# Attention scores as three split products, values held stationary, and the overflow branch ahead of the first pair of experts

## The chip, the cores and the metric

One core of a Trainium2 chip runs the whole kernel. The metric is the device time of one execution in microseconds (us), lower is better. The kernel's engines are TensorE (PE in the profile; PEld are its weight loads), VectorE (DVE), ScalarE (ACT), GpSimd (POOL) and SyncE (SP), which issues the large transfers.

## What is computed

Two transformer blocks follow each other. The first has two layers over 256 latent and 256 context tokens of width 1024; the second has one layer over the 256 latent tokens. A layer of the first block mixes tokens in three branches and then sends each token to two of 32 experts. Cut to what matters here:

```python
def diff_softmax_mix(q, k, v, lam):                 # 4 heads, two maps of 64 each
    s = einsum('bqhmd,bkhmd->bhmqk', q, k) * 64 ** -0.5
    p = softmax(s, axis=-1)
    w = p[:, :, 0] - lam * p[:, :, 1]
    return einsum('bhqk,bkhe->bqhe', w, v)

def neighbourhood_attention(q, k, v, k_ctx, v_ctx, rpb, rows):   # 8 heads of 64
    s = concatenate([s_window + bias, s_ctx], axis=-1)           # scaled scores
    p = softmax(s, axis=-1)
    return p_window @ v_window + p_ctx @ v_ctx

def hier_moe(x, ...):      # 2 of 32 experts for a token, 1024 -> 512 -> 1024
    hdn = silu(xb @ w_gate[e]) * (xb @ w_up[e])
    return hdn @ w_down[e]                          # times the token's weight, summed

def rope(x, pos):          # second block, dilated branch: cos and sin of pos * inv
```

All inputs and the output are fp32.

## The kernel before

**Dense products.** A weight arrives in fp32 and is split into a high and a low part of type fp32r (L153 on ScalarE, L155 on VectorE). Activations are kept split as well (`xh`, `xl`), so a dense product is three fp32r matmuls per piece: high by high, low by high, high by low (L229 to L231, L247 to L249). An fp32 matmul, where there is one, is carried out as two instructions, which the profile counts as two records.

**Attention.** In `mix`, q and k are kept as fp32 tiles `qT` and `kT`, features on partitions, two heads (or the two maps of a head) in the two halves of the partitions. A pair of score matmuls (L618 in the differential attention, L675 in the neighbourhood attention) uses each half as a row tile of 64 rows: 128 queries by 512 keys for latent tiles, 256 keys for context tiles. Layer 0 works on four token tiles (two latent, two context), layer 1 on the two latent ones. VectorE takes the maximum (L621, L691, with the bias added at L689), ScalarE the exponential (L624, L694, L696, L702), TensorE transposes the weights in blocks of 128 (L137, `T`), ScalarE copies them out as `wT` (L635, L708), and TensorE multiplies them with the values (L637, L710). At L710 the weights `wT` (128 keys by 128 queries) are loaded and the values of one head (64 columns) move; the sums are divided by the softmax sums at L712 and L713 for a whole token tile. `to_yT` (L717) then transposes the result. For each latent pair four small transfers on POOL's queue bring the bias tile `bt` (L686); `bt`, `wT` and other tiles share four buffers (tag `t2`).

The order of instructions on an engine comes from the framework's scheduler, by readiness and program order. Dense pieces of the next products stand between the steps of the attention. A helper, `issue_after(x)`, queues the instructions of its block behind `x`, those on `x`'s engine alone.

**Experts.** For each layer `load` (L1016) brings the weights of two experts in six transfers of 2 MB on SP's queue: two of gate, two of up, two of down. They go into buffers in turn (L949 to L954): seven in layer 0, nine in layer 1. `choose` and `gather` make the matrix of chosen tokens for four experts (L1022, L1048; for the first four L1038); `expert_pair` multiplies two experts at once in two column tiles of 64 (L966 with L968 for gate and up, L990 with L992 for down), and `scatter` (L1082, L1083) adds the result to the tokens. Eight groups of two pairs follow each other, their TensorE order being program order; the `scatter` of a pair is issued inside the next one, and the next group's `gather` inside the second pair (`fill`, L1195) except in the first group. `overflow` (L1112) is a branch on the largest count of tokens of an expert: its body, which works through tokens beyond 64 of an expert with a loop, is not entered for these inputs. Every engine loads the count (L1114) and takes the branch (L1115). It stands behind the first group (L1211): there the last `scatter` is drained, a down buffer is given to the body, the load of that buffer is issued after it (L1212), and the next group's `gather` follows.

**Rope tables.** `rope_tables` (L1336) makes cosines and sines for block 2's dilated branch. It is called in the idle time of the first norm (`idle`, L1729), two transfers for it in the setup.

Of the kernel before, what the change touches and what calls it, by code (L numbers as in the profile page):

```python
# [8 lines left out]
FT = mybir.dt.float32  # L9
BF = mybir.dt.bfloat16  # L10
FR = mybir.dt.float32r
I32 = mybir.dt.int32
# [77 lines left out]
class Builder:  # L90
# [173 lines left out]
    def setup(self, st, open_mix, load_x):  # L264
# [23 lines left out]
        with self.tp("setup", 1) as tp:  # L288
# [4 lines left out]
            inv = self.p_h.tile([128, 64], FT, name="inv2")  # L293
            nc.gpsimd.dma_start(inv, I["k_inv"])
            pi = self.p_h.tile([128, 2], I32, name="pi")
            nc.gpsimd.dma_start(pi, I["positions_2"][0].rearrange("(t p) -> p t", p=128))
            self.rope_in = inv, pi
# [110 lines left out]
    def mix_norm(self, tp, l, h, mid=None, junk=None, idle=None):  # L408
# [6 lines left out]
        for w in range(2):  # L415
            y = tp.tile([128, 2, D], FT, name="xs", tag="xs", bufs=2)
            r = self.stats(h, (2 * w, 2 * w + 1), y[:, 0] if junk is None else junk)
            if w == 0 and self.spare:
                self.fence.append(self.sq)
            for k in range(2):  # L420
                scaled = nc.vector.tensor_scalar(y[:, k], h[:, 2 * w + k], r[:, k:k + 1], None, op0=OP.mult)
            xs.append(y)
        if idle is not None:
            with self.tc.issue_after(scaled.ins):
                idle()
# [81 lines left out]
    def mix(self, l, xh, xl):  # L507
# [80 lines left out]
        rope = at.tile([128, 256], FT, name="rope")  # L588
        nc.gpsimd.dma_start(rope, I["k_rope"])

        def ev_qk(dst):
            def ev(t, ps):
# [8 lines left out]
                nc.scalar.activation(dst[:, :, t * 128:(t + 1) * 128], pt.rearrange("p (c t) -> p c t", c=4), AF.Copy)  # L601
# [5 lines left out]
        for t in tts:  # L607
# [4 lines left out]
            for h in range(4):  # L612
                S = [self.aux() for _ in range(2)]
                mx, nm, sm = (self.small(2, f"da{x}") for x in "xns")
                P = at.tile([128, 2, 512], FT, name="P", tag="P", bufs=2)
                for m in range(2):
                    r0 = m * 64
                    mm(S[m][:, :nk], lhsT=qT[r0:r0 + 64, h, t * 128:(t + 1) * 128], rhs=kT[r0:r0 + 64, h, k0:],  # L618
                       start=True, stop=True)
# [3 lines left out]
                for m in range(2):  # L623
                    nc.scalar.activation(P[:, m, :nk], S[m][:, :nk], AF.Exp, bias=nm[:, m:m + 1], scale=0.125,  # L624
                                         accum_out=sm[:, m:m + 1])
# [34 lines left out]
        self.dense_w(W(O_KC), 8, 512, xh, xl, 512, lambda c, ps: nc.scalar.activation(kT[:, c], ps, AF.Copy))  # L660
        self.dense_w(W(O_QC), 8, 512, xh, xl, n, lambda c, ps: nc.scalar.activation(qT[:, c, :n], ps[:, :n], AF.Copy))
        self.dense_x(W(O_VC), 8, 512, xh, xl, allt, lambda t, ps: nc.scalar.activation(v[:, t], ps, AF.Copy))
        yc = at.tile([128, 4, 512], FT, name="ytok", tag="ytok")
        for t in tts:
            po = self.aux()
            sm = self.small(8, "nsm")
# [3 lines left out]
            for h in range(8):  # L670
                c, r0 = h // 2, (h % 2) * 64
                if h % 2 == 0:
                    S2 = [self.aux() for _ in range(2)]
                    for m in range(2):
                        mm(S2[m][:, :nk], lhsT=qT[m * 64:m * 64 + 64, c, t * 128:(t + 1) * 128],  # L675
                           rhs=kT[m * 64:m * 64 + 64, c, k0:], start=True, stop=True)
                S = S2[h % 2]
                P = at.tile([128, 2, 512], FT, name="PC", tag="P", bufs=2)[:, 0]
                mx, nm, ps2 = (self.small(2, f"na{x}") for x in "xns")
                if lat:  # L680
                    if h % 2 == 0:
                        bt = at.tile([128, 2, 4, 64], FT, name="bt", tag="t2", bufs=4)
                        for u in range(2):
                            off = h * 889 + (3 - (2 * t + u)) * 127 + 63
                            for k in range(2):
                                nc.gpsimd.dma_start(bt[u * 64:(u + 1) * 64, k], bass.AP(  # L686
                                    tensor=self.d_bias.tensor, offset=self.d_bias[l].offset + off + k * 889,
                                    ap=[[7111, 64], [127, 4], [1, 64]]))
                    nc.vector.tensor_tensor_reduce(P[:, :256], S[:, :256], bt[:, h % 2].rearrange("p a b -> p (a b)"),  # L689
                                                   1.0, -3e38, OP.add, OP.max, mx[:, 0:1])  # L690
                    nc.vector.tensor_reduce(mx[:, 1:2], S[:, 256:], axis=AX.X, op=OP.max)  # L691
                    nc.vector.tensor_tensor(mx[:, 0:1], mx[:, 0:1], mx[:, 1:2], op=OP.max)
                    nc.vector.tensor_scalar(nm[:, 0:1], mx[:, 0:1], -0.125, None, op0=OP.mult)
                    nc.scalar.activation(P[:, :256], P[:, :256], AF.Exp, bias=nm[:, 0:1], scale=0.125,  # L694
                                         accum_out=ps2[:, 0:1])
                    nc.scalar.activation(P[:, 256:], S[:, 256:], AF.Exp, bias=nm[:, 0:1], scale=0.125,  # L696
                                         accum_out=ps2[:, 1:2])
                    nc.vector.tensor_tensor(sm[:, h:h + 1], ps2[:, 0:1], ps2[:, 1:2], op=OP.add)
                else:
                    nc.vector.tensor_reduce(mx[:, 0:1], S[:, :nk], axis=AX.X, op=OP.max)  # L700
                    nc.vector.tensor_scalar(nm[:, 0:1], mx[:, 0:1], -0.125, None, op0=OP.mult)
                    nc.scalar.activation(P[:, :nk], S[:, :nk], AF.Exp, bias=nm[:, 0:1], scale=0.125,  # L702
                                         accum_out=sm[:, h:h + 1])
                pt = self.aux()
                for b in range(nk // 128):
                    self.T(pt[:, b * 128:(b + 1) * 128], P[:, b * 128:(b + 1) * 128])
                wT = at.tile([128, 512], FT, name="wT", tag="t2", bufs=4)
                nc.scalar.activation(wT[:, :nk], pt[:, :nk], AF.Copy)  # L708
                for b in range(nk // 128):
# [50 lines left out]
    def tail(self, l, mh, ml, h_src, hook, emit):  # L760
# [426 lines left out]
        for bt in range(8):  # L1187
            PTw = []
            with in_order():
# [645 lines left out]
```

## Time and profile before

| | |
|---|---|
| median of 3 runs | 2613.09 us |
| lowest, highest | 2610.91, 2614.15 us |
| the profiled execution | 2611.69 us |
| its span in the trace | 2609.9 us |
| mean granted clock of TensorE | 0.98 |

The stages in that span, in rounded us: layer 0's mixing 30 to 610 (differential attention 183 to 300, neighbourhood attention 382 to 510), its projection and routing to 690, its experts 690 to 1183; layer 1's mixing 1200 to 1520 (differential attention 1286 to 1352, neighbourhood attention 1404 to 1497), projection and routing to 1573, experts 1573 to 2032; block 2 from 2040 to 2610.

In the rows below, times are us unless marked ns. A row of a timeline gives the start, the time until the last of its instructions ends, the engine, the line, the operation and how many. The ends of matmuls are modelled, so that one overlaps the next by a little. A row of groups gives the busy time, the mean of one instruction in ns, and the idle time of the engine ahead of it with what released it. A row of windows gives for each engine the busy time and instructions in a stretch.

### The profile page before, as it was taken

Reading aid. Unit: us, or ns where it says so; the run is one execution under the profiler, and the core shown is the slowest. Engines: PE = TensorE matmul, PEld = TensorE weight load, DVE = VectorE, ACT = ScalarE, POOL = GpSimd, SP = SyncE. Lnnn points to the kernel's source line nnn. Section 1 sums busy time; section 2 is a strip of 40 time slices with the busy share of each in tenths; the row PEclk is TensorE's granted clock in tenths of the full one; section 3 lists DMA queues with packets and bytes.
Section 4 is the critical chain, followed back from the end, with each engine's and each line's share of the span. In section 5 each row is a group of like instructions: output and inputs, shape, how many; then the busy total and the mean of one; then the engine's idle time right before and its main releaser. Section 6 shows DMA issues by size and latency. Waiting matters only on the chain. (4 is left out here: it accounts for less than half of the span.)

```text
span 2609.9 us, 33466 instructions
## 1 busy us (share of the span) xinstructions
PE 2471.3 (95%) x13560; PEld 1686.8 (65%) x13560; DVE 1309.2 (50%) x2640; ACT 852.0 (33%) x1504; POOL 163.2 (6%) x187
## 2 busy tenths in 40 slices
PE   7999999999889999997999978999898899998998
PEld 5766776677544444545878774444342798897997
DVE  5635523346444444548553463233232686657784
ACT  4334333424211111115444441111110534444663
POOL 1200002011200000003000210000000100001000
PEclk9999999999899999998999999999999999999999
DMA  9743544263889999985243478999999435535452
GB/s 316 214 162 114 169 146 122 93 209 149 329 342 417 419 417 418 418 356 193 73 133 104 139 300 328 421 421 421 421 421 413 164 119 194 177 122 184 152 188 99
DMA packets 177363, 652.47 MB, mean 250 GB/s; under 512 B 15174, under 2 KB 18778, under 8 KB 127666
## 3 DMA queue, kind: packets, MB, share of 16 engines
q1 hardware_dynamic: 169682, 626.97, 62.4%
q0 software_dynamic: 7520, 23.29, 3.0%
q8 instruction: 109, 1.79, 0.3%
q14 instruction: 52, 0.43, 0.0%
HBM read 644.42 MB, written 5.80 MB: 249 GB/s over the span
## 5 line engine op out<-in xcount | busy, mean ns | idle before, releaser
L155 DVE TENSOR_TENSOR wl<-raw,wh 128x1024 fp32r<-128x1024 f32 (+1 forms) x279 | 335.8, 1207 | 310.9 <-ACT wh L153 305.3
L966 PE MATMUL acc<-raw,xg 128*64 128x512 f32 x896 | 399.0, 596 | 19.6 <-DMA raw<-in_moe_w_up 10.1
L153 ACT ACTIVATE wh<-raw 128x1024 fp32r<-128x1024 f32 (+1 forms) x288 | 299.0, 1045 | 334.9 <-PE acc L248 167.3
L968 PE MATMUL acc<-raw,xg 128*64 128x512 f32 x896 | 399.2, 596 | 0.0
L247 PE MATMUL acc<-xh,wh 128*128 128x256 f32 (+1 forms) x1184 | 370.6, 315 | 0.0
L248 PE MATMUL acc<-xl,wh 128*128 128x256 f32 (+1 forms) x1184 | 369.5, 313 | 0.0
L249 PE MATMUL acc<-xh,wl 128*128 128x256 f32 (+1 forms) x1184 | 368.5, 312 | 0.1
L966 PEld LDWEIGHTS acc<-raw,xg 128*64 128x64 f32 x896 | 119.8, 137 | 273.4 <-issue 247.2
L247 PEld LDWEIGHTS acc<-xh,wh 128*128 128x128 f32 x1184 | 226.3, 192 | 28.1 <-issue 13.8
L248 PEld LDWEIGHTS acc<-xl,wh 128*128 128x128 f32 x1184 | 226.4, 191 | 15.8 <-issue 5.9
L249 PEld LDWEIGHTS acc<-xh,wl 128*128 128x128 f32 x1184 | 225.9, 191 | 11.7 <-issue 1.0
L229 PE MATMUL acc<-wh,xh 128*128 128x512 f32 x544 | 214.0, 394 | 5.0 <-DVE xh L441 2.5
L230 PE MATMUL acc<-wl,xh 128*128 128x512 f32 x544 | 213.6, 393 | 0.3 <-DVE wl L155 0.3
L231 PE MATMUL acc<-wh,xl 128*128 128x512 f32 x544 | 213.8, 394 | 0.0
L990 PE MATMUL acc<-raw,hT 128*64 128x512 f32 x472 | 209.8, 596 | 3.0 <-ACT hT L982 3.0
L992 PE MATMUL acc<-raw,hT 128*64 128x512 f32 x472 | 209.8, 596 | 0.0
L997 DVE TENSOR_TENSOR aux<-aux,g 128x512 f32<-128x512 f32 x128 | 83.3, 694 | 185.7 <-PE aux L1083 185.7
L1108 DVE SCALAR_TENSOR_TENSOR yl<-acc,ws,yh 128x512 fp32r<-128x512 f32 x64 | 48.0, 750 | 214.6 <-ACT yh L1107 214.6
L990 PEld LDWEIGHTS acc<-raw,hT 128*64 128x64 f32 x472 | 61.8, 137 | 122.7 <-issue 115.3
L982 ACT ACTIVATE hT<-aux 128x512 f32<-128x512 f32 x32 | 19.1, 598 | 332.3 <-PE aux L137 332.3
L229 PEld LDWEIGHTS acc<-wh,xh 128*128 128x128 f32 x544 | 102.4, 188 | 31.8 <-issue 3.7
L968 PEld LDWEIGHTS acc<-raw,xg 128*64 128x64 f32 x896 | 119.8, 137 | 0.0
(479 smaller groups left out, 4303.0 us busy)
## 6 DMA issues: line engine op xcount, KB each, us to landing
raw<-in_moe_w_gate SPq DMA_DIRECT2D x59, 2048.0 KB
raw<-in_moe_w_down SPq DMA_DIRECT2D x59, 2048.0 KB
raw<-in_moe_w_up SPq DMA_DIRECT2D x53, 2048.0 KB
raw<-in_w_in SPq DMA_DIRECT2D x42, 2048.0 KB
raw<-in_w_ada SPq DMA_DIRECT2D x22, 2048.0 KB
rawx<-in_moe_w_up SPq DMA_DIRECT2D x11, 2048.0 KB
raw<-in_w_branch SPq DMA_DIRECT2D x18, 1024.0 KB
raw<-in_w_gate SPq DMA_DIRECT2D x6, 2048.0 KB
```

What stands on the lines that cost most here:

```text
L153: nc.scalar.activation(hi, src, AF.Copy)
L155: eng.tensor_tensor(lo, src, hi.bitcast(FT), op=OP.subtract)
L229: mm(ps[t][:, :W], lhsT=a, rhs=wh[:, jj, :W], start=j == 0, stop=False)
L230: mm(ps[t][:, :W], lhsT=a, rhs=wl[:, jj, :W], start=False, stop=False)
L231: self.last_mm = mm(ps[t][:, :W], lhsT=b, rhs=wh[:, jj, :W], start=False, stop=j == J - 1)
L247: mm(ps[c][:, :n], lhsT=a, rhs=xh[:, j, :n], start=j == 0, stop=False)
L248: mm(ps[c][:, :n], lhsT=a, rhs=xl[:, j, :n], start=False, stop=False)
L249: mm(ps[c][:, :n], lhsT=b, rhs=xh[:, j, :n], start=False, stop=j == J - 1)
L966: mm(ps[0:64], lhsT=xg[:, j, a0:a0 + 64], rhs=wa(j), start=j == 0, stop=j == 7)
L968: mm(ps[64:128], lhsT=xg[:, j, b0:b0 + 64], rhs=wb(j), start=j == 0, stop=j == 7)
L990: mm(py[half][0:64], lhsT=hT[:, c, 0:64], rhs=da(c, half), start=c == 0, stop=c == 3)
L992: mm(py[half][64:128], lhsT=hT[:, c, 64:128], rhs=db(c, half), start=c == 0, stop=c == 3)
```

## The change

1. q and k of both attentions are kept split in fp32r parts; a pair's scores are three products per row tile, the two tiles in turn. `issue_after` names an exponential.
2. In the neighbourhood attention the weights are normalised before they are transposed; the values are the loaded operand (128 keys by 64), `wT` moves, and the two heads of a pair go to two column tiles. The result comes out transposed and is split directly.
3. `overflow` stands ahead of the first pair, with five of its six loads issued before it; the first group gathers for the next one like the others and has no drain.
4. The rope tables are made in block 2's dilated stage; their inputs are loaded with block 2's constants.
5. The scratch for POOL's transfer descriptors is set to 2048 bytes, and some tiles share or get buffers of their own.

```diff
@@ mix: q, k and the scores
-            return (at.tile([128, 4, 512], FT, name="qT", tag="qT"),
-                    at.tile([128, 4, 512], FT, name="kT", tag="kT"))
+            return [[at.tile([128, 4, k], FR, name=f"{x}{p}", tag=f"{x}{p}") for p in "hl"]
+                    for x, k in (("q", n), ("k", 512))]
...
+        def scores(c, t, k0):
+            S = [self.aux() for _ in range(2)]
+            nk = 512 - k0
+            with ExitStack() as es:
+                if scored:
+                    es.enter_context(tc.issue_after(scored.pop().ins))
+                for i, (a, b) in enumerate(((0, 0), (1, 0), (0, 1))):
+                    for m in range(2):
+                        r = slice(m * 64, m * 64 + 64)
+                        mm(S[m][:, :nk], lhsT=qT[a][r, c, t * 128:(t + 1) * 128], rhs=kT[b][r, c, k0:],
+                           start=i == 0, stop=i == 2)
+            return S
...
-                nc.scalar.activation(dst[:, :, t * 128:(t + 1) * 128], pt.rearrange("p (c t) -> p c t", c=4), AF.Copy)
+                self.hilo(*(d[:, :, t * 128:(t + 1) * 128] for d in dst), pt.rearrange("p (c t) -> p c t", c=4))
...
-                S = [self.aux() for _ in range(2)]
+                S = scores(h, t, k0)
...
-                for m in range(2):
-                    r0 = m * 64
-                    mm(S[m][:, :nk], lhsT=qT[r0:r0 + 64, h, t * 128:(t + 1) * 128], rhs=kT[r0:r0 + 64, h, k0:],
-                       start=True, stop=True)
...
+                scored[:] = [e]
@@ mix: neighbourhood attention (the bias, maximum and exponential as before, per head m)
+                S2 = scores(c, t, k0)
...
+                    scored[:] = [e]
+                    nc.vector.reciprocal(ps2[:, 0:1], ps2[:, 0:1])
+                    nc.vector.tensor_scalar(P[:, :nk], P[:, :nk], ps2[:, 0:1], None, op0=OP.mult)
                     pt = self.aux()
                     for b in range(nb):
                         self.T(pt[:, b * 128:(b + 1) * 128], P[:, b * 128:(b + 1) * 128])
                     wT = at.tile([128, 512], FT, name="wT", tag="t2", bufs=4)
                     nc.scalar.activation(wT[:, :nk], pt[:, :nk], AF.Copy)
...
-                    mm(po[:, h * 64:(h + 1) * 64], lhsT=wT[:, b * 128:(b + 1) * 128],
-                       rhs=v[:, k0 // 128 + b, h * 64:(h + 1) * 64], start=b == 0, stop=b == nk // 128 - 1)
-            nc.vector.reciprocal(sm, sm)
-            nc.vector.tensor_tensor(yc[:, t].rearrange("p (h d) -> p h d", h=8), po.rearrange("p (h d) -> p h d", h=8),
-                                    sm[:, :, None].to_broadcast([128, 8, 64]), op=OP.mult)
+                for b in range(nb):
+                    for m in range(2):
+                        h = 2 * c + m
+                        mm(po[m * 64:m * 64 + 64, c * 128:(c + 1) * 128],
+                           lhsT=v[:, k0 // 128 + b, h * 64:(h + 1) * 64], rhs=wTs[m][:, b * 128:(b + 1) * 128],
+                           start=b == 0, stop=b == nb - 1)
+            nc.scalar.activation(yc[:, :, t * 128:(t + 1) * 128], po.rearrange("p (c q) -> p c q", c=4), AF.Copy)
...
-        yh, yl = self.to_yT(yc, n)
+        for c in range(4):
+            self.hilo(yh[:, c], yl[:, c], yc[:, c, :n])
@@ experts
-        raws = load(0)
+        raws = load(0, 5)
         P2 = choose(0)
         xg = gather(0, P2)
         slot_weights()
+        overflow(raws[5])
+        nc.sync.dma_start(self.pairs(raws[5]), dsrc(0, 1))
...
-                    if 0 < bt < 7:
+                    if bt < 7:
                         ahead.append(gather(bt + 1, choose(bt + 1)))
...
-                if bt in (0, 7):
+                if bt == 7:
                     for part in range(2):
                         scattered = scatter(*before, part)
...
-                before = None
-                raws = load(4, 5)
-                overflow(raws[5])
-                nc.sync.dma_start(self.pairs(raws[5]), dsrc(4, 1))
                 hook()
-                P2 = choose(1)
-                xg = gather(1, P2)
-            elif bt < 7:
+            if bt < 7:
                 raws = load(bt * 4 + 4)
                 xg = ahead.pop()
@@ rope
+        cosT, sinT = self.rope_tables(dl, self.inv, self.pos)
...
-        nc.scalar.activation(sinT, a, AF.Sin)
+        nc.scalar.activation(sinT[:, :, 1], a, AF.Sin)
+        nc.scalar.activation(sinT[:, :, 0], a, AF.Sin, scale=-1.0)
         nc.scalar.activation(cosT, m, AF.Sin)
...
-    nc = bacc.Bacc("TRN2", target_bir_lowering=False, num_devices=1)
+    nc = bacc.Bacc("TRN2", target_bir_lowering=False, num_devices=1, dynamic_dma_scratch_size=2048)
```

## Rows read from the trace of the kernel before

**Rows 1.** Page, part 1: busy us (share of the span) and instructions of each engine.

```profile
PE 2471.3 (95%) x13560; PEld 1686.8 (65%) x13560; DVE 1309.2 (50%) x2640; ACT 852.0 (33%) x1504; POOL 163.2 (6%) x187
```

**Rows 2.** Windows, first-block attention: us, then each engine's busy us (instructions), PEclk, DMA share, GB/s.

```profile
383.00:510.00 127.00, 126.65 (x639) 83.46 (x637) 45.37 (x155) 55.03 (x151) 16.37 (x27) 1.00 0.31 96
...
510.00:554.00 44.00, 44.00 (x217) 31.19 (x218) 18.70 (x24) 14.75 (x20) 6.09 (x10) 1.00 0.63 208
...
1480.00:1500.00 20.00, 16.18 (x85) 13.15 (x84) 6.73 (x21) 7.96 (x20) 4.48 (x7) 0.77 0.55 173
```

**Rows 3.** Windows, experts of layer 1: before pair 0, and near the end.

```profile
1575.00:1580.00 5.00, 5.00 (x26) 1.61 (x24) 0.00 (x0) 0.00 (x0) 0.00 (x0) 1.00 0.35 102
...
1900.00:2000.00 100.00, 88.72 (x418) 34.60 (x416) 27.65 (x56) 11.48 (x18) 1.46 (x2) 1.00 1.01 421
```

**Rows 4.** Waits of TensorE, 1573 to 2032 us: us in total, times, longest.

```profile
PE acc L966 <- DMA raw<-in_moe_w_up: 10.1, 7, 4.5
PE acc L966 <- DMA raw<-in_moe_w_gate: 9.2, 8, 1.7
```

**Rows 5.** Groups by line, engine PE: count, busy us, mean ns, idle before and its releaser.

```profile
L710 PE MATMUL aux<-vv,wT 128*128 128x64 f32 x320 | 45.7, 285 | 1.2 <-ACT wT L708 1.2
...
L675 PE MATMUL aux<-kT,qT 64*128 64x512 f32 (+1 forms) x96 | 39.8, 570 | 0.0
...
L618 PE MATMUL aux<-kT,qT 64*128 64x512 f32 (+1 forms) x96 | 32.6, 570 | 0.0
```

**Rows 6.** Timeline, PE, around two score groups: start, us, engine, line, count.

```profile
382.17 0.39 PE L230 MATMUL acc<-wl,xh 128*128 128x512 f32 x1
382.39 0.39 PE L231 MATMUL acc<-wh,xl 128*128 128x512 f32 x1
382.71 1.13 PE L675 MATMUL aux<-kT,qT 64*128 64x512 f32 x4
383.77 0.64 PE L361 MATMUL acc<-raw,condT 128*32 128x512 f32 x4
...
390.30 1.12 PE L675 MATMUL aux<-kT,qT 64*128 64x512 f32 x2
391.35 1.10 PE L710 MATMUL aux<-vv,wT 128*128 128x64 f32 x8
```

**Rows 7.** Timeline, PE, experts: first instructions of groups, the gap, and layer 1's start.

```profile
690.29 0.64 PE L966 MATMUL acc<-raw,xg 128*64 128x512 f32 x1
...
752.29 1.09 PE L137 MATMUL aux<-glob,ws 128*128 128x128 f32 x4 [5.35 <-DVEq L1115]
...
762.51 0.64 PE L966 MATMUL acc<-raw,xg 128*64 128x512 f32 x1
...
819.54 0.59 PE L966 MATMUL acc<-raw,xg 128*64 128x512 f32 x1
...
879.89 0.59 PE L966 MATMUL acc<-raw,xg 128*64 128x512 f32 x1
879.90 0.59 PE L968 MATMUL acc<-raw,xg 128*64 128x512 f32 x1
880.32 0.59 PE L966 MATMUL acc<-raw,xg 128*64 128x512 f32 x1
...
1573.48 0.64 PE L966 MATMUL acc<-raw,xg 128*64 128x512 f32 x1
```

**Rows 8.** Page, part 5: a VectorE operation of 512 columns.

```profile
L997 DVE TENSOR_TENSOR aux<-aux,g 128x512 f32<-128x512 f32 x128 | 83.3, 694 | 185.7 <-PE aux L1083 185.7
```

**Rows 9.** Bias transfers: timeline of POOL, layer 1; page part 6, us to landing.

```profile
1435.84 2.44 POOL L686 DMA_DIRECT2D bt<-d_bias  x4 [9.16 <-issue]
...
bt<-d_bias POOLq DMA_DIRECT2D x64, 64.0 KB, 2.4
```

**Rows 10.** Line L1115: duration ns min/median/max, first and last start.

```profile
L1115 PEldq COMPARE_BRANCH  x2: 344/1840/3337, 745.9 to 1624.0; - x2
```

**Rows 11.** Timeline, ACT, at the start: a table load.

```profile
12.14 1.28 ACT L1359 ACT_TABLE_LOAD   x1
```

More of the change, by code (lines that the diff above doesn't have):

```diff
@@ L406, in stats, with mix_norm @@
         return self.rsqrt(ss, 1.0 / D, EPS)
-    def mix_norm(self, tp, l, h, mid=None, junk=None, idle=None):
+    def mix_norm(self, tp, l, h, mid=None, junk=None):
         nc = self.nc
@@ L420, in mix_norm @@
             for k in range(2):
-                scaled = nc.vector.tensor_scalar(y[:, k], h[:, 2 * w + k], r[:, k:k + 1], None, op0=OP.mult)
+                nc.vector.tensor_scalar(y[:, k], h[:, 2 * w + k], r[:, k:k + 1], None, op0=OP.mult)
             xs.append(y)
-        if idle is not None:
-            with self.tc.issue_after(scaled.ins):
-                idle()
         order = [(w, j) for w in range(2) for j in range(0, 8, 2)]
@@ L583, in attn_tiles @@
         def attn_tiles():
-            return (at.tile([128, 4, 512], FT, name="qT", tag="qT"),
-                    at.tile([128, 4, 512], FT, name="kT", tag="kT"))
+            return [[at.tile([128, 4, k], FR, name=f"{x}{p}", tag=f"{x}{p}") for p in "hl"]
+                    for x, k in (("q", n), ("k", 512))]
         qT, kT = attn_tiles()
-        rope = at.tile([128, 256], FT, name="rope")
+        scored = []
+        def scores(c, t, k0):
[10 more added lines that the diff above has]
+            return S
+        rope = at.tile([128, 2, 512], FT, name="rope", tag="P", bufs=2)[:, 0, :256]
         nc.gpsimd.dma_start(rope, I["k_rope"])
@@ L623, in mix @@
                 for m in range(2):
-                    nc.scalar.activation(P[:, m, :nk], S[m][:, :nk], AF.Exp, bias=nm[:, m:m + 1], scale=0.125,
-                                         accum_out=sm[:, m:m + 1])
+                    e = nc.scalar.activation(P[:, m, :nk], S[m][:, :nk], AF.Exp, bias=nm[:, m:m + 1], scale=0.125,
+                                             accum_out=sm[:, m:m + 1])
+                scored[:] = [e]
                 nc.vector.reciprocal(sm, sm)
@@ L669, in mix @@
             nk = 512 - k0
[L670 to L673, printed above, removed]
-                    for m in range(2):
[L675 to L709, printed above, removed]
-                    mm(po[:, h * 64:(h + 1) * 64], lhsT=wT[:, b * 128:(b + 1) * 128],
-                       rhs=v[:, k0 // 128 + b, h * 64:(h + 1) * 64], start=b == 0, stop=b == nk // 128 - 1)
@@ L716, in mix @@
+            nc.scalar.activation(yc[:, :, t * 128:(t + 1) * 128], po.rearrange("p (c q) -> p c q", c=4), AF.Copy)
         self.gate_branch(1, W2(w_in, O_GATE), I["w_branch"][l, 0], xh, xl, yh, yl, n, merged)
-        yh, yl = self.to_yT(yc, n)
+        yh = self.p_y.tile([128, 4, n], FR, name="yh", tag="yh")
+        yl = self.p_y.tile([128, 4, n], FR, name="yl", tag="yl")
+        for c in range(4):
+            self.hilo(yh[:, c], yl[:, c], yc[:, c, :n])
         self.gate_branch(2, W2(w_in, O_GATE + 2048), I["w_branch"][l, 2], xh, xl, yh, yl, n, merged)
@@ L1279, in mix2_consts @@
         self.ggbc = bp.tile([128, 128], FT, name="ggbc")
-        self.sin2 = bp.tile([128, 2, 2, 64], FT, name="sin2")
-        nc.vector.tensor_scalar(self.sin2[:, :, 0], self.rope2[1], -1.0, None, op0=OP.mult)
-        nc.vector.tensor_copy(self.sin2[:, :, 1], self.rope2[1])
+        self.inv = bp.tile([128, 64], FT, name="inv2")
+        nc.gpsimd.dma_start(self.inv, I["k_inv"])
+        self.pos = bp.tile([128, 2], I32, name="pi")
+        nc.gpsimd.dma_start(self.pos, I["positions_2"][0].rearrange("(t p) -> p t", p=128))
         wal = bp.tile([128, 8, 16], FT, name="wal")
@@ L1336, in rope_tables @@
     def rope_tables(self, rp, inv, pi):
-        nc, I, c = self.nc, self.I, self.p_const
-        cosT = c.tile([128, 2, 64], FT, name="cosT")
-        sinT = c.tile([128, 2, 64], FT, name="sinT")
+        nc = self.nc
+        cosT = rp.tile([128, 2, 64], FT, name="cosT")
+        sinT = rp.tile([128, 2, 2, 64], FT, name="sinT")
         pf = rp.tile([128, 2], FT, name="pf")
@@ L1375, in blk_mix @@
         uinc, ones = blk[:, 1792:1920], blk[:, 1920:2048]
-        cosT, sinT = self.rope2[0], self.sin2
         gp = ExitStack()
@@ L1728, in mid @@
                     jobs.append(self.prep(hp))
-                def idle():
-                    self.rope2 = self.rope_tables(hp, *self.rope_in)
-                    nc.scalar.activation(hp.tile([128, 1], FT, name="tab"), self.rope2[0][:, 1, 0:1], AF.Tanh)
-                xh, xl = self.mix_norm(hp, 0, h, mid, idle=idle)
+                xh, xl = self.mix_norm(hp, 0, h, mid)
                 jobs[0]()
```

54 lines of the change are left out of this document (42 added, 12 removed).

## The prediction

> **What bounds the kernel now.** First the page's list of busy times: TensorE works for 95% of the span [rows 1]. So work taken off TensorE counts, but only where nothing else ends last; I therefore read one table of windows per stage and then the transfers.
>
> In the first layer's neighbourhood attention TensorE is busy 126.65 of 127 us, and the dense work behind it fills 44.00 of 44 us [rows 2]: there is always a dense product to put in a gap, so TensorE time saved there is saved in full. In the second layer the same loop ends with TensorE busy only 16.18 of 20 us [rows 2]: the filler has run out and the chain scores, softmax, transposes, values sets the end. In the experts of layer 1 the picture is different again: from 1900 to 2000 us TensorE is busy 88.72 of 100 us while the DMA engines are at 1.01 of their share at 421 GB/s [rows 3], and the list of waits of TensorE in that stage is led by weights, 10.1 + 9.2 us [rows 4]. This stage ends when its loads end. Block 2 is not touched, except by the rope tables.
>
> **Scores.** The two score lines draw 39.8 + 32.6 us [rows 5] for 192 records, 48 pairs of heads. Where both row tiles of a pair stand together, four records take 1.06 us from their start to the next instruction's (drawn 1.13); where other work stands between, one tile's two records take 1.05 (drawn 1.12) [rows 6]. Without the 6% of overlapping tail the 72.4 us are 68. After: three fp32r products per tile. One such product of 512 columns follows the last after 0.22 us (I take 0.23), 0.32 at the turn to the row tiles [rows 6]. Together: 3 x 0.23 + 0.1 = 0.79 instead of 1.06; apart: about 1.56 instead of 2.10. Both are a quarter less: 68 x 0.255 = 17.3 us (differential 7.8, neighbourhood 9.5). Bounds: 3 us (the tiles of a pair stay apart, with a turn each) to 35 us (all come together). I keep a quarter, since the helper only orders ScalarE's instructions: the one it names is an exponential, and a matmul is on another queue.
>
> **Values stationary.** Eight records of one head take some 1.03 us (drawn 1.10) [rows 6]; 45.7 us drawn [rows 5], less the same tail of 0.07 per group of eight, is 43; some records overlap neighbours more, so I take 39. After, a record moves 128 columns instead of 64, but two column tiles run together. The experts' product shows that pair: its two tiles start 0.01 us apart (L966, L968), and the next record of 512 columns follows after 0.43 us [rows 7]; a quarter of that for 128 columns is 0.11, near the present 1.03 / 8 = 0.13. Half the slots: -19.5 us. Bounds -2 (the tiles take turns) to -21. The output comes out transposed, so 24 transposes go, records of 128 columns too, at 0.13: -3.1.
>
> **Where this lands.** Layer 0 has 8 latent and 8 context pairs per line, layer 1 eight latent ones: weights 12 and 8, so 60% and 40%. Layer 0: 0.6 x (17.3 + 19.5) + 2.1 = 24.2. What is added lies on VectorE and ScalarE: splitting q and k, some 30 subtractions, and 48 normalisations, at 0.69 us per 512 columns [rows 8] over 50 us; VectorE is busy only 45.37 of 127 us there [rows 2], so dense matmuls cover it. Without that cover each pair would cost some 1.4 us, 22 us over 16 pairs. I take **-23** (-7 to -36). Layer 1, differential: 0.4 x 7.8 = **-3** (0 to -7). Layer 1, neighbourhood: TensorE saves 12.7 us, but the chain ends it. The chain's own change per pair: + two normalisations of at most 0.69, half beside the other head, so +0.7; + a reciprocal, 0.1; - half of the last values product, 0.5. Eight pairs x 0.3 = **+2**. The table's bias tiles wait as before: POOL idles 9.16 us before it issues four, 2.44 us [rows 9], because their buffer is shared with the weights that the values product reads. Bounds: -12 (all TensorE time saved) to +10 (the whole normalisation on the chain).
>
> **Branch in layer 0.** Now group 0 takes 690.29 to 762.51 = 72.2 us, group 1 to 819.54 = 57.0, group 2 to 879.89 = 60.4 [rows 7]. The first is long because the scatter drains before the branch, TensorE waits 5.35 us for VectorE's side of it, and the next tokens are gathered with nothing beside [rows 7]. After, group 0 is as group 1 (no scatter before it) and the rest as group 2: 72.2 becomes 60.4, -11.8. To pay: branch and count load on each queue. TensorE's two branches took 344 and 3337 ns [rows 10]; I give the longer to layer 0. At most 2.4 of it is uncovered, as the gather's eviction runs beside: **-11** (-8.4 to -11.8). The Trainium skill (Runtime: NRT & Kernel Launch, section Instruction fetch mechanics) says that a taken branch out of the fetched window waits for a fetch. The trace agrees with one long and one short branch; by that rule both layers could pay 3.3, some 3 us more than my sum.
>
> **Branch in layer 1.** SP issues five loads, then the copy of the down weights whose buffer the branch body uses, and it has to wait for TensorE to pass the branch. All later loads are queued behind it on SP. Now nine buffers are filled before pair 0: four loads beyond the five; then the transfers stand still (DMA 0.35 of 1575 to 1580, so they restart at about 1578.2) [rows 3]. After, these four come behind the branch. A load is 2.097 MB, at 421 GB/s 5.0 us [rows 3]; four are 20 us. TensorE passes the branch when the gather is issued, at the place where pair 0 starts now, 1573.48 [rows 7], up to 3.3 us later; with 1 us for the first packets the transfers restart at 1574.5 to 1578 instead of 1578.2, and the pause at the old branch (about 1.5) goes. Since loads end this stage: 20 - 2.2 - 1.5 = **+16** (+10 if SP gets two loads ahead of the waiting one, +18). In layer 0 the same delay is covered: 91 loads x 5.0 from 692 end by 1150, and eight groups (57.0 + 7 x 60.4 = 480 us from 690) need the last by about 1160, a down product's last half ahead of their end.
>
> **Rope tables.** Now at the start, hidden. After, two table loads of 1.28 [rows 11] and three sines on ScalarE, estimated at 3.5 us in all, and their VectorE steps, in block 2 beside its matmuls, plus two POOL transfers in the setup: **+1** (-0.2 to +4, uncovered). The descriptor scratch frees memory and costs nothing so far as POOL's transfers fit in it.
>
> **Sum.** -23 - 3 + 2 - 11 + 16 + 1 = -18. The profiled execution took 2611.69 us (span 2609.9): 2593.7. It lies 1.4 under the median of 2613.09, so **2595**. A change under 0.2% (5 us) can't be told from none.
>
> **Rivals.**
> - *Loads not delayed* (12%): if SP's copy waits for less than TensorE, or TensorE is still the limit in layer 1, the experts there give -9 (layer 0's 11.8 with the full branch paid) instead of +16: 2570. Against it stand the waits on weights [rows 4].
> - *All pairs together* (11%): scores near the 35 us bound, should the named exponential keep a pair's products together after all, 35 - 17.3 = 17.7 us more, four fifths of it on the path, 14, and layer 1's loop at -8 instead of +2: 2571.
> - *Layer 0 follows its chain too* (14%): longer chains use up the filler and -23 becomes -8: 2610, no change. Against: 44 us of dense work remain behind the loop [rows 2].
> - *Tiles take turns* (7%), slower: if row and column tiles did not run beside each other in the new order, scores lose two thirds of their gain and the values nearly all: -18 becomes about +1. If each also paid the 0.09 us seen at the turn to row tiles [rows 6], the new records (48 x 6 + 320 = 608) x 0.09 x 3/4 on the path add 41: 2655. It decides from 0.01 us per record. Against it: L966 and L968 start together [rows 7], four score records take 1.06 [rows 6].
> - *POOL's issues wait for room* (6%), slower: the smaller scratch could make each of a pair's four bias transfers wait for the one before: 4 x (0.61 + 2.4) = 12.0 instead of 2.44 + 2.4 [rows 9], +7 on the chain of eight layer-1 pairs, +57: 2651. It decides from +2.2 us per pair. No row shows POOL waiting for room now.
>
> The Trainium skill (TensorEngine Tiling (Array Packing), section Key Properties) states that a change of tiling mode, not of the tile, drains TensorE; that speaks for the turns, since values now change mode as scores do. The trace agrees in kind: 0.32 us at such a turn against 0.22 [rows 6]; paid once per group the rule adds 80 x 0.1 = 8 us, not 41.
>
> **Numbers.** My case has 50% (own range 2582 to 2606). Range 2567 to 2616: both fast cases and the layer-0 chain are inside, the two slow ones out. Faster: 50 + 12 + 11, less what of my case lies above 2608, plus a little of the chain case: 0.72; same 0.15; slower 0.13.
>
> **What would show it.** Right: score groups of six records near 0.8 us, values records of two column tiles starting together, a first layer-0 group of 57 us, in layer 1 the DMA engines still for some 20 us more ahead of pair 0, and its last expert load some 16 us later against the start of pair 0. Wrong: TensorE idle in the first layer's attention, loads flowing before the branch, bias transfers over 5 us apart, or values records over 0.13 us each.

## The result, and the profile after

The changed kernel takes 2569.05 us (median of 4, 2568.77 to 2569.47) against 2613.62 (2610.91 to 2615.92) for the kernel before on the same chip: a ratio of 0.983, interval 0.9813 to 0.9847, so 44.6 us faster. The forecast was 18 us faster. 2569.05 lies in the range, near its lower end, but the change is two and a half times the one forecast; two of the rivals gave 2570 and 2571, but neither of them is what happened.

Where the 42.7 us of the two spans (2609.9 and 2567.2) went, by stages from the first matmul of a stage to the first of the next in each profiled execution:

| stage | before | after | change | forecast |
|---|---|---|---|---|
| start to the first score of layer 0 | 183.4 | 176.4 | -7.0 | 0 |
| first score to the first expert pair, layer 0 | 506.9 | 489.8 | -17.1 | -23 |
| first pair to the start of group 7, layer 0 | 431.0 | 419.5 | -11.5 | -11 |
| from there to the first score of layer 1 | 165.1 | 164.7 | -0.4 | 0 |
| first score to the first expert pair, layer 1 | 287.1 | 281.0 | -6.1 | -1 |
| experts of layer 1, to block 2's first transposes | 473.0 | 471.5 | -1.5 | +16 |
| block 2 | 563.5 | 564.4 | +0.9 | +1 |

The largest miss is a loss that did not come: layer 1's experts.

The page of the changed kernel, against [rows 1]:

```profile
PE 2437.5 (95%) x13632; PEld 1670.9 (65%) x13632; DVE 1339.0 (52%) x2752; ACT 854.8 (33%) x1510; POOL 162.7 (6%) x187
```

and the groups of its values (L721) and of its score line (L593, three products), with count, busy us and mean ns, against [rows 5]:

```profile
L721 PE MATMUL aux<-wT,vv 128*64 128x128 f32 x320 | 34.3, 297 | 0.5 <-ACT wT L716 0.2
L593 PE MATMUL aux<-kh,qh 64*128 64x512 f32 (+1 forms) x96 | 26.5, 464 | 0.0
L593 PE MATMUL aux<-kh,ql 64*128 64x512 f32 (+1 forms) x96 | 24.8, 381 | 0.0
L593 PE MATMUL aux<-kl,qh 64*128 64x512 f32 (+1 forms) x96 | 24.4, 412 | 0.0
```

The three rows of L593 overlap one another (two tiles run at once), so they can't be added. Counted from each start to the next start of any matmul, and without one idle stretch of 3.4 us, the scores take 53.8 us instead of 67.5, and the values 32.6 instead of 39.4. TensorE is at 95% as before.

How one pair looks now is seen in the timeline of TensorE, the answer to [rows 6]:

```profile
370.12 0.49 PE L593 MATMUL aux<-kh,qh 64*128 64x512 f32 x2
370.45 0.39 PE L593 MATMUL aux<-kh,ql 64*128 64x512 f32 x2
370.68 0.40 PE L593 MATMUL aux<-kl,qh 64*128 64x512 f32 x2
371.01 1.92 PE L356 MATMUL acc<-raw,condT 128*32 128x512 f32 x16
...
376.90 0.43 PE L721 MATMUL aux<-wT,vv 128*64 128x128 f32 x2
377.26 0.50 PE L593 MATMUL aux<-kh,qh 64*128 64x512 f32 x2
377.60 0.39 PE L593 MATMUL aux<-kh,ql 64*128 64x512 f32 x1
377.93 1.09 PE L721 MATMUL aux<-wT,vv 128*64 128x128 f32 x14
378.94 0.50 PE L593 MATMUL aux<-kh,ql 64*128 64x512 f32 x1
378.95 0.73 PE L593 MATMUL aux<-kl,qh 64*128 64x512 f32 x2
```

A pair's six score products together take 371.01 - 370.12 = 0.89 us (forecast 0.79, before 1.06). A values group takes 0.36 for its first two records, which stand apart, and 1.01 for the other fourteen: 1.37 us for both heads, where the forecast's halving meant about 1 and before took 2.06. 21 of the 24 values groups are split like this.

The experts, against [rows 7]; the timeline's first instructions of groups 0, 1 and 2 of layer 0, and of layer 1's first group:

```profile
666.16 0.61 PE L978 MATMUL acc<-raw,xg 128*64 128x512 f32 x1 [0.30 <-PEq L1127]
...
723.93 0.64 PE L978 MATMUL acc<-raw,xg 128*64 128x512 f32 x1
...
784.23 0.59 PE L978 MATMUL acc<-raw,xg 128*64 128x512 f32 x1
...
1531.38 0.61 PE L978 MATMUL acc<-raw,xg 128*64 128x512 f32 x1 [0.30 <-PEq L1127]
```

Group 0 takes 57.8, group 1 60.3: the forecast's step. TensorE's idle time at the branch is 0.30 us in each layer, so the branch itself is nearly free in this kernel. (In two of the kernels below it is not.)

SP's timeline in layer 1 shows what the forecast had wrong (L971 is `load`, L1198 the load that waits for the branch):

```profile
1487.53 0.37 SPq L971 DMA_DIRECT2D raw<-in_moe_w_down  x1
1507.20 0.37 SPq L971 DMA_DIRECT2D rawx<-in_moe_w_gate  x1
1507.62 0.46 SPq L971 DMA_DIRECT2D raw<-in_moe_w_gate  x1
1508.12 0.47 SPq L971 DMA_DIRECT2D raw<-in_moe_w_up  x1
1531.20 0.38 SPq L1198 DMA_DIRECT2D raw<-in_moe_w_down  x1
1535.06 0.37 SPq L971 DMA_DIRECT2D raw<-in_moe_w_up  x1
```

Three loads of the second pair, written behind the branch in the source, are issued 23 us before the load that waits for it: the framework's scheduler put them ahead of the branch on SP. Of the four loads that the forecast had waiting, one waits. Loads flowing before the branch was one of the signs that the prediction named for being wrong.

### The profile page after: what moved, and what is told of

It is laid out like the page before. It is cut to its first block, busy times and chain, and to the rows that moved or that the text cites. A ratio compares the mean times of both kernels' runs of the same rounds, so it can differ in the third digit from the quotient of the medians.

```text
span 2567.2 us, 33740 instructions
## 1 busy us (share of the span) xinstructions
PE 2437.5 (95%) x13632; PEld 1670.9 (65%) x13632; DVE 1339.0 (52%) x2752; ACT 854.8 (33%) x1510; POOL 162.7 (6%) x187
```

## The experiments

All stand against the same kernel before; "stage" means the stages of the table above.

### The loads held behind the branch

```diff
-        nc.sync.dma_start(self.pairs(raws[5]), dsrc(0, 1))
+        last_down = nc.sync.dma_start(self.pairs(raws[5]), dsrc(0, 1))
...
-                raws = load(bt * 4 + 2)
+                with tc.issue_after(last_down.ins) if l and bt == 0 else ExitStack():
+                    raws = load(bt * 4 + 2)
```

> The changed kernel with all loads of layer 1's second pair issued behind the load that waits for the branch (in the changed kernel three of them stand ahead of it). Theory 1: those three loads, 5 us each, are why the experts of layer 1 did not lose what was forecast; behind the branch the transfers end 15 us later against the start of pair 0, and the kernel takes 2584 us (2581 to 2586). Theory 2: with the first group shorter TensorE sets the end of that stage, not the transfers; then it stays within 3 us of 2569.

2582.5 us (2580.06 to 2582.72), 13.5 more than the changed kernel. The whole difference is in layer 1's experts, 485.7 instead of 471.5 us; no other stage moved by over 1.5. SP's timeline of this kernel:

```profile
1486.32 0.37 SPq L971 DMA_DIRECT2D raw<-in_moe_w_down  x1
1529.96 0.38 SPq L1198 DMA_DIRECT2D raw<-in_moe_w_down  x1
1530.40 0.46 SPq L971 DMA_DIRECT2D rawx<-in_moe_w_gate  x1
1530.90 0.47 SPq L971 DMA_DIRECT2D raw<-in_moe_w_gate  x1
```

So the transfers rest. In the 18 us from the issue of the three loads on, the DMA share (the last number but one) is 0.95 in the changed kernel and 0.10 in this one:

```profile
1508.00:1526.00 18.00, 4.25 (x32) 4.05 (x32) 14.48 (x59) 7.00 (x11) 5.25 (x4) 0.64 0.95 380
```

```profile
1507.00:1525.00 18.00, 4.43 (x32) 4.27 (x33) 14.27 (x59) 6.85 (x11) 5.04 (x4) 0.64 0.10 31
```

TensorE's waits in that stage (us in total, times, longest), of this kernel:

```profile
PE acc L978 <- DMA raw<-in_moe_w_up: 17.1, 14, 4.9
PE acc L978 <- DMA raw<-in_moe_w_gate: 15.8, 16, 1.4
```

and of the changed kernel:

```profile
PE acc L978 <- DMA raw<-in_moe_w_up: 13.1, 9, 4.9
PE acc L978 <- DMA raw<-in_moe_w_gate: 11.1, 11, 1.4
```

With four loads behind the branch the stage is 12.7 us longer than before the change: that is the forecast's +16, a little smaller. So the mechanism holds, and the issue order decides whether it acts. By the forecast's own sum one waiting load gives 5.0 - 2.2 - 1.5 = +1.3, where -1.5 was measured: in both cases the sum is some 3 us too high.

### The branch alone, and the rest without it

The first kernel is the one before with only the branch moved (and with it the drain and the gather of the first group; own tiles for its body, the smaller scratch); the second is the changed kernel with the branch back behind the first group.

```diff
# branch: on the kernel before
+        overflow(raws[5])
+        nc.sync.dma_start(self.pairs(raws[5]), dsrc(0, 1))
...
# attn: on the changed kernel
-        overflow(raws[5])
-        nc.sync.dma_start(self.pairs(raws[5]), dsrc(0, 1))
...
+                raws = load(4, 5)
+                overflow(raws[5])
...
```

> The kernel before with only the branch ahead of the first pair (with its own tiles for the branch body and the smaller descriptor scratch). Theory 1: -11.6 in layer 0's experts, -1 in layer 1's, since three loads stand ahead of the branch here too: 2612.4 - 12.5 = 2600 us, less if TensorE's half clock falls elsewhere. Theory 2 (the early branch costs what the loads show only in this kernel): +15 in layer 1, 2616 us.

> The changed kernel with the overflow branch back behind the first group (attention, rope tables and scratch as changed). Theory 1: the branch's place is worth 11.5 us in layer 0 and 1 in layer 1: 2569 + 12.5 = 2581.5 us. Theory 2 (as forecast, the early branch loses 16 us in layer 1's experts, and something else made this up): without it the kernel is 5 us faster, 2564 us.

2602.7 us (2601.21 to 2603.76; ratio 0.9961, 0.9946 to 0.9976) and 2577.66 us (2576.31 to 2578.84). The branch is worth 10.1 us alone and 8.6 beside the rest, less than the 12.5 expected of both. The experts are as expected: -11.5 and -1.1 alone, -11.6 and -1.2 beside the rest. The missing 2.4 and 3.9 us lie mostly ahead of layer 0's first pair: 510.2 with the branch there and 506.9 without it, and beside the rest 489.8 and 486.4. That time comes from two things.

One is the granted clock of TensorE, which falls towards its lower level of 1.2 GHz in short dips. Two windows from about the same work, the first of the changed kernel, the second of the kernel of the experiment before, which has the same source in layer 0 (PEclk is the third number from the end):

```profile
580.00:594.00 14.00, 14.00 (x71) 11.71 (x70) 8.05 (x17) 4.81 (x6) 2.11 (x4) 0.88 0.46 171
```

```profile
579.00:593.00 14.00, 14.00 (x79) 11.81 (x78) 9.32 (x19) 5.28 (x6) 2.11 (x4) 1.00 0.54 195
```

TensorE is busy all the time in both, for 71 records instead of 79. A second dip of the changed kernel, against the one without the branch there:

```profile
629.00:639.00 10.00, 9.08 (x41) 7.58 (x41) 6.28 (x10) 3.08 (x7) 7.42 (x3) 0.83 0.42 142
```

```profile
626.00:636.00 10.00, 9.04 (x50) 7.47 (x49) 7.82 (x11) 4.60 (x9) 8.96 (x5) 1.00 0.29 80
```

Five kernels here share the changed kernel's source for layer 0 from the first score to the first pair. In the profile of the changed kernel, with both dips, that stage takes 489.8 us; in three of the others, with one dip each, 488.2 to 488.5; in the last, the later broadcast (below), with none (PEclk 1.00 from 176 to 640 us), 487.0. So the dips come and go with the branch in the same place; each costs some 1.4 us, and what is left for the branch is 487.0 - 486.4 = 0.6.

The other is the branch itself. In the kernel before with the branch moved, TensorE idles 1.95 us at layer 0's first pair, where the changed kernel idles 0.30; so does one more kernel, with fp32 scores (below), whose rows are these, the branch in ns (min/median/max of two) and the first pair:

```profile
L1127 PEldq COMPARE_BRANCH  x2: 767/2052/3337, 680.5 to 1553.3; - x2
684.12 0.61 PE L978 MATMUL acc<-raw,xg 128*64 128x512 f32 x1 [1.97 <-PEq L1127]
```

and the changed kernel's branch:

```profile
L1127 PEldq COMPARE_BRANCH  x2: 353/359/365, 664.2 to 1528.1; - x2
```

TensorE's branch takes 3.3 us in the one and 0.35 in the other, in the same place of the source; what makes it long no run shows. The kernel before with the branch moved has two dips in this stage, at 615 and 660 us, and the kernel before one, at 614. One dip more (1.4) and the 1.95 us of idle time are together its 3.3 us.

### The branch ahead of the first gather

```diff
         P2 = choose(0)
-        xg = gather(0, P2)
         slot_weights()
         overflow(raws[5])
         nc.sync.dma_start(self.pairs(raws[5]), dsrc(0, 1))
+        xg = gather(0, P2)
```

> The changed kernel with the branch ahead of the first gather instead of behind it. Theory 1 (the transfers set the end of layer 1's experts, and they stand still until TensorE passes the branch): the waiting load starts some 6 us sooner against pair 0, -5 us, 2564 us; nothing in layer 0, which is bound by TensorE. Theory 2: the gather now waits behind the branch, and TensorE loses up to 3 us in each layer with nothing back: 2569 to 2575.

2571.15 us (2570.13 to 2572.6), no gain. Layer 1's experts took 469.0 us instead of 471.5, so the load did start sooner, but layer 0 lost 5.7 ahead of its first pair. TensorE's wait for VectorE's side of the branch, ahead of layer 0's gather (2.9 us in the changed kernel, for another step of VectorE):

```profile
PE aux L1050 <- DVEq L1127: 10.6, 1, 10.6
```

So the same edit was made for layer 1 alone:

```diff
+        if not l:
+            xg = gather(0, P2)
         slot_weights()
         overflow(raws[5])
         nc.sync.dma_start(self.pairs(raws[5]), dsrc(0, 1))
+        if l:
+            xg = gather(0, P2)
```

> The changed kernel with the branch ahead of the first gather in layer 1 alone (in both layers, the gather of layer 0 waited 10.6 us for VectorE's side of the branch, and the kernel was 2 us slower). Theory 1: layer 1's experts, bound by transfers, keep the 2.5 us that they gained and lose 0.9 ahead of pair 0: 2567.5 us (2566 to 2568.5). Theory 2: no gain beyond the scatter of the runs: 2569 to 2570 us.

2565.33 us (2562.65 to 2565.75; ratio 0.9815, 0.9802 to 0.9829), under every run of the changed kernel, though the runs stand in another comparison and the intervals of the two ratios overlap. Its load behind the branch is issued at 1525.68 instead of 1531.20, layer 1's experts take 468.6 us, and 1.3 are lost ahead of the first pair.

### Scores and values one at a time

The first kernel is the changed one with each score as one fp32 product of unsplit q and k; the second has the values moving, the sums divided once per tile and `to_yT` again.

```diff
# fp32scores
-                for i, (a, b) in enumerate(((0, 0), (1, 0), (0, 1))):
+                for i, (a, b) in enumerate(((0, 0),)):
...
# tokvalues
+                mm(po[:, h * 64:(h + 1) * 64], lhsT=wT[:, b * 128:(b + 1) * 128],
+                   rhs=v[:, k0 // 128 + b, h * 64:(h + 1) * 64], start=b == 0, stop=b == nk // 128 - 1)
...
```

> The changed kernel with the scores as one fp32 product from unsplit q and k. Theory 1 (TensorE's time decides in layer 0 and in layer 1's differential attention): 13 us of TensorE time come back, some 8 in layer 0's mixing and 2 to 3 in layer 1's: 2579.5 us. Theory 2 (the chains decide, and the subtractions that split q and k lie on them): 4 us slower at most, 2569 to 2573.

> The changed kernel with the neighbourhood attention's values moving again (weights loaded, sums divided once per tile, 24 transposes back). Theory 1 (TensorE's time): 7 us for the values and 3 to 4 for the transposes, three fifths of it in layer 0, in layer 1 only a part: 8 us slower, 2577 us. Theory 2 (layer 1's loop follows its chain): layer 1 gets 3 us faster without the normalisations, layer 0 6 slower: 2572 us.

2591.13 us (2589.39 to 2592.75): the kernel with fp32 scores is 22 us slower, twice what I expected. By stages: 12.8 in layer 0 from the first score on, of which 1.7 are the long branch shown above, so 11.1 for the scores; 5.5 in layer 1's mixing (3.1 from the first score of the differential attention to the first of the neighbourhood attention, 0.5 in the neighbourhood loop, 1.9 behind it); and 5.1 before the first score, where there is no score at all (next experiment). 2574.54 us (2570.86 to 2575.17): the stationary values are worth 5.5 us, 7.4 in layer 0, and in layer 1 they cost 1.5: its neighbourhood loop takes 90.4 us from first score to last values, 88.0 with moving values, 92.0 before the change. There the chain is longer with stationary values; as the run takes back the normalisation and the joint values product of two heads together, it does not tell which of the two lengthens it.

The order that the change names with `issue_after` in the scores has no part in this: built without it, the changed kernel is the same program.

### The start

The rope tables alone moved, on the kernel before (the hunks of the diff that name them), and then, also on the kernel before, two single edits: the scratch, and the scratch with a gain vector in a tile of its own.

```diff
# scr
+    nc = bacc.Bacc("TRN2", target_bir_lowering=False, num_devices=1, dynamic_dma_scratch_size=2048)
# gbc: scr, and
-        gbc = at.tile([128, 128], FT, name="gbc")
+        gbc = self.small(128, "gbc")
```

> The kernel before with only the rope tables moved to block 2. Theory 1: the 7 us by which the changed kernel is ahead at its first score come from this part (waits of TensorE of 2.5 us at 51 us and 2.4 us at 135 us, the second with a stretch at half clock behind it): 7 less 0.5 in block 2, 2607 us, and both waits gone. Theory 2: the tables were hidden as forecast, and the waits went with another part of the change: 2614 us, both waits still there.

> The kernel before with only the smaller descriptor scratch. Theory 1: POOL's transfers never fill it, no difference: 2613 us within 2 us, the four bias transfers issued in 2.4 us as before. Theory 2: issues wait for room, layer 1's neighbourhood attention gets longer, 2616 us or more.

> The kernel before with the small scratch, and the broadcast of the sub-norm gain (gbc) into a tile of its own that is free from the start, so that POOL issues it long before 110 us, not at 121.7 where it meets the bias row (brow) that a later TensorE wait of 2.4 us hangs on. Theory 1: that meeting delays the row (10.5 us from issue to use here, 8.2 where the gain is loaded at 110): the wait and the half clock behind it go, start of the first score 4 us earlier, 2609 us. Theory 2: the row is late for another reason, the wait stays: 2613 us.

The rope tables: 2608.51 us (2606.97 to 2611.95; ratio 0.9988, 0.9978 to 0.9997), some 3 to 4 us, in the profiled execution all of it before the first score (179.7 instead of 183.4); block 2 is the same (563.4). The scratch: 2614.58 us, ratio 1.0001 (0.9992 to 1.001), nothing. The gain vector: 2608.91 us, ratio 0.9985 (0.9975 to 0.9994), some 4 us. Both intervals end just under 1. The first score of the gain vector's profile does not show it: it comes at 184.0 us, at 183.4 in the kernel before, and at 186.8 with the scratch alone, so single profiles differ by 3 us in this stage. The profiles part early: POOL writes a row out (`d_rows`, L394) at 104.20 us before, 107.72 with the scratch and 109.07 with the gain vector. From there to the first score it is 79.2, 79.1 and 75.0 us, so 4 less with the gain vector. The waits of TensorE from 25 us to the first score tell the two edits apart (us in total, times, longest); the kernel before:

```profile
PE acc L229 <- DVE xh L441: 2.5, 1, 2.5
PE acc L229 <- ACT row L386: 2.4, 1, 2.4
```

with the rope tables moved, where the first is gone (as in all kernels here that have them moved, while all four that have them at the start show 2.5 us):

```profile
PE acc L229 <- ACT row L381: 2.9, 1, 2.9
```

with the gain vector loaded early, where the second is gone:

```profile
PE acc L229 <- DVE xh L441: 2.5, 1, 2.5
PE acc L230 <- DVE wl L155: 0.3, 1, 0.3
```

and the changed kernel, which has neither:

```profile
PE acc L230 <- DVE wl L155: 0.3, 1, 0.3
```

The second wait is for a small row of the modulation's bias (`brow`). In the kernel before, POOL issues the broadcast of the gain vector and the rope table for the attention at 121.7 and 122.3 us, beside the row's own load at 122.9, and the row is used 10.5 us after its issue. The changed kernel issues the broadcast at 109.8 and the rope table at 116.9, its row's load is at 119.8, and the row is used 8.2 us after it. In the kernel with the gain vector's own tile, too, both are early (the rope table at 117.6, the row's load at 127.5), and the row takes 8.2; so the runs do not tell which of the two transfers delays the row. What frees the broadcast's buffer sooner in the changed kernel is the split of q and k with its tiles: with fp32 scores, all else as changed, the broadcast is back at 119.35, the row at 11.05 and the wait at 2.9. This is where most of the 5.1 us lay that the fp32 scores lost before the first score.

A last run tried it from the other side, with the broadcast later in the changed kernel:

```diff
+        kr = nc.gpsimd.dma_start(rope, I["k_rope"])
+        with tc.issue_after(kr.ins):
+            nc.gpsimd.dma_start(gbc, bcast(I["da_subln_g"][l]))
```

> The changed kernel with that broadcast (gbc) issued behind the rope table's transfer, at some 117 to 118 us instead of 109.8. Theory 1: it meets the bias row again, the row takes 10 us or more, TensorE waits 2 to 3 us at 130 us: 2573 us. Theory 2: no difference, 2569 us.

2569.04 us, no difference; but the edit missed its aim. The broadcast came at 117.44, still 2.2 us ahead of the row's load, and the row took 8.2 us. So it does not show how close they must come.

### Both gains together

Layer 1 with moving values and the branch ahead of its first gather, layer 0 as changed.

> The changed kernel with the branch ahead of the first gather in layer 1, and in layer 1 the values moving again (sums divided once per tile); layer 0 as changed. Theory 1: with moving values layer 1's loop ended 1.5 us sooner, as its chain holds no normalisation; it adds to the 3.7 us of the early branch: 2564 us, against 2565.3 for the branch alone. Theory 2: the loop's end only moves the filler about, 2565 to 2566 us.

2564.41 us (2563.36 to 2565.43; ratio 0.9813, 0.98 to 0.9827), not to be told from the 2565.33 of the early branch alone. The run of the later broadcast, 2569.04, stands in the same comparison; against it the two edits together gain 4.6 us. The loop did get shorter (88.3 us against 89.8), and 78.9 instead of 77.7 us then pass to the first pair: the filler has moved behind the loop, and little is left.

## Why the prediction was wrong, point by point

- **Branch in layer 1**, +16 forecast, -1.5 measured: the step that failed. "All later loads are queued behind it on SP" took the source's order for the queue's. Three loads stand ahead of the branch. Held back, they give 14.2 us, and the stage is 12.7 us longer than before. The term allowed for two loads ahead, at +10, though by its own sum two waiting loads give 10.0 - 3.7 = +6; it did not allow for three. The rival *Loads not delayed* came out at 2570 against 2569.05, but that is luck: its -9 in this stage was -1.5, the copy does wait for TensorE, the transfers do end the stage, and the rest of the number came from the terms below.
- **Branch in layer 0**, -11 forecast, -11.5 measured in the experts: right. TensorE pays 0.30 us at the branch in the changed kernel, whose two branches take 353 and 365 ns, and 1.95 and 1.97 us in the two kernels where the long branch (3317 and 3337 ns) stands in the new place too. So the forecast's "At most 2.4 of it is uncovered" was fair, and that the changed kernel pays so little is luck as far as these runs show. The Trainium skill (Runtime: NRT & Kernel Launch, section Instruction fetch mechanics) says that a taken branch out of the fetched window waits for a fetch; the traces agree in that the same branch is long or short, and the long one cost 1.65 us more, but none shows the fetch.
- **Rope tables**, +1 forecast, -3.7 in the start and nothing in block 2: the term was mis-sized because it was looked for at the new place only. "Now at the start, hidden" was not read from a row; TensorE's waits at the start have one, 2.5 us on `xh` from VectorE, and it goes when the tables are moved.
- **What no term held**: the wait for the bias row, 2.4 us and the lower clock behind it, which the changed kernel no longer has, as its tiles let the broadcast start sooner.
- **Scores**, 17.3 us of TensorE time forecast, 13.7 counted: six products take 0.89 us instead of 0.79, and a part stands apart. In layer 0 this gave 11.1 us, where 10.4 was the share, in layer 1's differential attention 3.1, as forecast. The rival *All pairs together* did not happen: the named exponential changes nothing in the program.
- **Values**, 19.5 forecast, 6.9 counted, 7.4 in layer 0 with the transposes where 13.8 was the share: "half the slots" holds for the fourteen records that stand together (1.01 us, or 0.07 each), not for the group, which is split and pays turns twice; the context tiles' groups of eight records take 0.36 + 0.58 us, hardly less than the 1.03 of eight records before. The Trainium skill's rule that a change of tiling mode drains TensorE (TensorEngine Tiling (Array Packing), section Key Properties) points the way of this; the trace agrees with 0.36 us for two records that stand alone between other modes, some 0.2 more than two of the fourteen. For the values the prediction priced a turn at 0.1 us, once per group, and left it out of its sum; the trace has two turns in most groups.
- **Layer 0's mixing as a whole**, -23 forecast, -17.1 measured: scores and values gave 18.5; one dip of the clock more than before (1.4) and the branch ahead of the first pair (0.6) take about 2 back.
- **Layer 1's neighbourhood loop**, +2 forecast, -1.6 measured: that stationary values lengthen it was right (moving values are 2.4 us shorter there). The split scores give only 0.5 of the gain (the loop takes 90.9 us with fp32 scores, 90.4 with split ones, 92.0 before); where the rest comes from no run shows. Another 1.5 us went behind the loop, where the forecast had no term.

Summed, the stages are off by -17.5 (experts of layer 1), -7 (the start), -5 (mixing of layer 1) and, the other way, +6 (mixing of layer 0): together some -24 of the 24.7 us between the change of the spans, -42.7, and the forecast, -18.

## What to carry to other kernels

Read the order of a queue from the built program, not from the source: a load written behind a branch may be issued ahead of it, and that was worth 13 us here. When a stage ends with its transfers, count the loads that can be in flight before the point that waits, and move that point ahead in this stage alone. When a block of work is moved, list what waited at its old place, and look at what else a new layout of buffers lets start sooner.

## What was not expected of the hardware

A small transfer with others beside it was late by 2 to 3 us: a bias row was used 8.2 us after its issue where POOL's broadcast and rope table had been issued 2.2 us or more before it, and 10.5 to 11.1 us after where both came within 1.2 us. TensorE's wait of 2.4 us behind it in the kernel before was followed by matmuls of 512 columns at 0.43 us each instead of 0.23, here in the timeline of TensorE, which adds some 1.6 us to the wait:

```profile
134.84 0.50 PE L229 MATMUL acc<-wh,xh 128*128 128x512 f32 x1 [2.43 <-ACT row L386]
...
136.47 0.63 PE L231 MATMUL acc<-wh,xl 128*128 128x512 f32 x1
136.90 0.63 PE L229 MATMUL acc<-wh,xh 128*128 128x512 f32 x1
...
139.28 0.40 PE L229 MATMUL acc<-wh,xh 128*128 128x512 f32 x1
```

The second and third row are 0.43 us apart; at 139.28 the matmuls are at 0.23 again. But the wait does not always bring this: with the rope tables moved, TensorE waits 2.94 us at the same place, and the same matmuls run at 0.23 behind it:

```profile
132.72 0.50 PE L229 MATMUL acc<-wh,xh 128*128 128x512 f32 x1 [2.94 <-ACT row L381]
133.06 0.40 PE L230 MATMUL acc<-wl,xh 128*128 128x512 f32 x1
133.29 0.40 PE L231 MATMUL acc<-wh,xl 128*128 128x512 f32 x1
```

And the clock fell in the changed kernel at 588 us with TensorE busy throughout (the window of 580 to 594 us above). So a difference of 1 to 3 us between single profiles can be such a dip, and is read beside the granted clock.
